# A one-core encoder trunk: how a Strassen FFN transfers its weight sums, and its second column block as a plain product

## The chip, the cores and the metric

The kernel runs on one core of a Trainium2 chip as one launch. The metric is the device time in microseconds (us), the median of three runs.

## The reference

Two requests of 256 tokens each (512 tokens in all, width 1024) go through two layers. A layer is a half-step SwiGLU FFN, a token mixer, and a second half-step FFN; all in float32.

```
def swiglu(x, wg, wu, wd):
    return (jax.nn.silu(x @ wg) * (x @ wu)) @ wd
...
    for l in range(DEPTH):
        x = x + 0.5 * swiglu(rmsnorm(x, ffn1_norm[l]), ffn1_wg[l], ffn1_wu[l], ffn1_wd[l])
        h = rmsnorm(x, mix_norm[l])
        ...
        x = x + merged @ w_out[l]
        x = x + 0.5 * swiglu(rmsnorm(x, ffn2_norm[l]), ffn2_wg[l], ffn2_wu[l], ffn2_wd[l])
```

`wg` and `wu` are 1024 x 2816, `wd` is 2816 x 1024. The four calls of the FFN are named FFN 1 to FFN 4 here, in order of time.

## The kernel before, in words

**Precision.** Each float32 operand is split into a rounded high part and the rest (`split`, lines 218 to 229: ACT copies the high part `wh`, line 226; DVE subtracts it and leaves `wl`, line 228). A product is three matmuls: high x high, high x low, low x high.

**The FFN** (`ffn`, from line 339). The normed input lies transposed in `xT` = (`xth`, `xtl`), 8 slices of 128 channels by 512 tokens. The 22 column tiles of `wg` and `wu` are worked off in pairs, 11 blocks, in three stages (tiles 0 to 7, 8 to 15, 16 to 21); after each stage `rowproj` (lines 295 to 336) multiplies by the matching rows of `wd`. Before, block 0 is a plain product (`proj`, lines 235 to 242: for a 128-column weight tile, 8 slices x 3 matmuls; in block 0 in two halves of 256 tokens). The ten other blocks call `seven` (lines 393 to 443), a Strassen scheme (Winograd form). It takes the weights as a 2 x 2 matrix whose rows are the channel halves and whose columns are gate and up, and the activations as channel halves by token halves. So W11 is the upper half of `wg`, W21 the lower half of `wg`, W22 the lower half of `wu`. It makes seven products of 24 matmuls with 256 columns (`product`, lines 384 to 391), in the order W11, t2, t1, t3, W21, W22, and the second t2; the block ends with vector work for silu and the gate (lines 420 to 443).

**The activation side** (`combos`, lines 355 to 374) is made once in each FFN. Four tiles `q` are filled by a transfer of the high part (SP's queue, line 361) and an accumulating transfer of the low part (POOL's queue, line 362); four subtractions on DVE (line 363) make the sums, and these are split into `C[5]`, `C[6]`, `C[7]`, `C[3]` (lines 370, 371). `C[5]` and the negated `C[4]` are written in place into the second token half of `xT`, so all of `xT` must have been read by then.

**The weight side** in `seven`: the sums t1 and t3 come by transfer. SP loads t1's first addend and W22 into the two halves of a `raw` tile (lines 399, 400), POOL adds the upper half of `wu` onto t1 (line 401); t3 goes as two halves into the tiles P and M, loaded by SP (line 406) and added onto by POOL (line 407). W11 and W21 go in halves into tiles S and R. DVE makes t2 = t1 + W22 (line 416), and adds W21 onto it later (line 431).

**What sets the order.** Every engine and each transfer queue works in the order of its instructions. A scheduler fixes that order when the program is built, from priorities and its own timing. The loads and splits of a block have a priority that puts them up to a block ahead. `raw` has 2 tiles, `wh` and `wl` 4 each, P and M 2 each. A tile is reused when its last reader is done.

Of the kernel before, what the change touches and what calls it, by code (L numbers as in the profile page):

```python
# [13 lines left out]
F32 = mybir.dt.float32  # L14
F32R = mybir.dt.float32r
# [45 lines left out]
def trunk_kernel(tc, I, O, dbg=None, depth=DEPTH, stop=None):  # L61
    nc = tc.nc
    with ExitStack() as st:
# [22 lines left out]
        def uv(shape=(P, 2, TOK), dt=F32):  # L86
            return pv_.tile(list(shape), dt, tag="v", name=nm("v"))
# [4 lines left out]
        def dtmp(tag, shape=(P, H, P)):  # L92
            return pd.tile(list(shape), F32, tag=tag, name=nm(tag))
# [245 lines left out]
        def ffn(wg, wu, wd, xT, after, extra=None, norm=None):  # L339
# [15 lines left out]
            def combos():  # L355
                q = {}
                for g, c in enumerate((g0, g1)):
                    for k, r in enumerate((low, high)):
                        q[g, k] = u((P, 4, 256))
                        with tc.high_priority(offset=100):  # L360
                            nc.sync.dma_start(q[g, k], xh[:, r, c].bitcast(F32))
                            G_.dma_start(q[g, k], xl[:, r, c].bitcast(F32), accum_op=ALU.add)
                sub = lambda o, i, j: V.tensor_tensor(o, i, j, op=ALU.subtract)
                sub(q[1, 1], q[1, 0], q[1, 1])
                sub(q[1, 0], q[1, 0], q[0, 0])
                sub(q[0, 0], q[0, 0], q[1, 1])
                sub(q[0, 1], q[0, 1], q[0, 0])
                for n, f, dst in ((5, q[1, 1], [t[:, low, g1] for t in xT]), (6, q[0, 0], None), (7, q[1, 0], None), (3, q[0, 1], None)):
                    hi, lo = C[n] = dst or [uv((P, 4, 256), F32R) for _ in range(2)]
                    A.copy(hi, f)  # L370
                    V.tensor_tensor(lo, f, hi.bitcast(F32), op=ALU.subtract)  # L371
                C[4] = [t[:, high, g1] for t in xT]
                for t in C[4]:
                    A.activation(t, t.bitcast(F32), AF.Copy, scale=-1.0)
# [9 lines left out]
            def product(ps, w, act, start=True):  # L384
                (wh, wl), (ch, cl) = w, act
                for j in range(2):
                    m, o = slice(j * P, (j + 1) * P), ps[:, j, :]
                    for k in range(4):
                        T.matmul(o, wh[:, k, m], ch[:, k, :], start=start and j + k == 0, stop=False, skip_group_check=True)  # L389
                        T.matmul(o, wh[:, k, m], cl[:, k, :], start=False, stop=False, skip_group_check=True)  # L390
                        T.matmul(o, wl[:, k, m], ch[:, k, :], start=False, stop=k == 3, skip_group_check=True)  # L391

            def seven(f, hh, hl):
                c = slice(f * P, f * P + 256)
                rows = lambda w, k0, n: w[k0 * P:(k0 + n) * P, c].rearrange("(k p) n -> p k n", p=P)
                with tc.high_priority(offset=AHEAD):
                    r = pr.tile([P, 2048], F32, tag="raw", name=nm("raw")).rearrange("p (q k n) -> p q k n", q=2, k=4)
                    w11, w22, t1_ = [dtmp("S", (P, 2, 256)) for _ in range(2)], r[:, 1], r[:, 0]
                    nc.sync.dma_start(t1_, rows(wg, 0, 4))
                    nc.sync.dma_start(w22, rows(wu, 4, 4))  # L400
                    G_.dma_start(t1_, rows(wu, 0, 4), accum_op=ALU.add)
                    for i, t in enumerate(w11):
                        nc.sync.dma_start(t, rows(wg, 2 * i, 2))
                    t3 = [dtmp(n, (P, 2, 256)) for n in "PM"]
                    for i, t in enumerate(t3):
                        nc.sync.dma_start(t, rows(wu, 4 + 2 * i, 2))
                        G_.dma_start(t, rows(wu, 2 * i, 2), accum_op=ALU.add)
                    w21 = [dtmp("R", (P, 2, 256)) for _ in range(2)]
                    for i, t in enumerate(w21):
                        nc.sync.dma_start(t, rows(wg, 4 + 2 * i, 2))  # L410
                sq_ = (P, 2, 256)
                X, E, Z = bank("f", sq_), bank("d", sq_), bank("a", sq_)
                product(X, parts_of(w11), X11)
                with tc.high_priority(offset=AHEAD):
                    t2 = u((P, 4, 256))
                    V.tensor_tensor(t2, t1_, w22, op=ALU.add)
                p1s, G = dtmp("C", sq_), dtmp("E", sq_)
                A.copy(p1s, X)
                product(E, parts_of([t2]), C[6])
                V.tensor_tensor(G, E, p1s, op=ALU.subtract)  # L420
                product(Z, parts_of([t1_]), C[5])
                product(E, parts_of(t3), C[7], False)
                H, y22 = dtmp("B", sq_), tmp(sq_)
                V.tensor_tensor(H, E, p1s, op=ALU.subtract)
                V.tensor_tensor(y22, Z, H, op=ALU.add)
                product(X, parts_of(w21), X12, False)
                s0 = tmp(sq_)
                A.activation(s0, X, AF.Silu)
                with tc.high_priority(offset=AHEAD):
                    for i, t in enumerate(w21):  # L430
                        V.tensor_tensor(t2[:, 2 * i:2 * i + 2, :], t2[:, 2 * i:2 * i + 2, :], t, op=ALU.add)
                product(Z, parts_of([w22]), C[3], False)
                V.tensor_tensor(G, Z, G, op=ALU.add)
                V.tensor_tensor(s0, s0, G, op=ALU.mult)
                product(E, parts_of([t2]), C[4], False)
                y21 = dtmp("B", sq_)
                V.tensor_tensor(y21, p1s, E, op=ALU.subtract)
                A.activation(y21, y21, AF.Silu)
                V.tensor_tensor(y22, y21, y22, op=ALU.mult)
                for v, g in ((s0, g0), (y22, g1)):  # L440
                    hi, lo = hh[-1][:, :, g], hl[-1][:, :, g]
                    A.copy(hi, v)
                    V.tensor_tensor(lo, v, hi.bitcast(F32), op=ALU.subtract)

            for f0, f1 in ((0, 8), (8, 16), (16, 22)):
                hh, hl = [], []
                for f in range(0, f1 - f0, 2):
                    hh.append(u(dt=F32R))
                    hl.append(u(dt=F32R))
                    if f0 + f:  # L450
                        seven(f0 + f, hh, hl)
                        continue
                    bs = [bank_alt() for _ in range(4)]
                    if norm is not None:
                        ws = []
                        norm(0)
                        for i, (b, rv) in enumerate(zip(bs, raw0)):
                            hi = pw.tile([P, 8, P], F32R, tag="whi", name=nm("wh"))
                            lo = pw.tile([P, 8, P], F32R, tag="wlo", name=nm("wl"))
                            if i:  # L460
                                k = (3, 7, 7)[i - 1]
                                A.copy(hi[:, 0, :1], xT[0][:, k, :1])
                                V.tensor_copy(lo[:, 0, :1], xT[1][:, k, :1])
                            ws.append(split(rv, (hi, lo), off=0 if i else AHEAD))
                            proj(b, ws[-1], xT, 0, 256)
                        norm(1, [w[0][:, 0, :1].bitcast(F32) for w in ws])
                        for b, w in zip(bs, ws):
                            proj(b, w, xT, 256, 512)
                    else:
                        gs, us = wcols(wg, 0), wcols(wu, 0)  # L470
                        for g in range(2):
                            for b, w in zip(bs, (gs[0], us[0], gs[1], us[1])):
                                proj(b, w, xT, g * 256, g * 256 + 256)
                    combos()
                    for j in range(2):
                        gate(bs[2 * j], bs[2 * j + 1], f + j, hh, hl)

                if extra is not None and f1 == 22:
                    extra()

                def src(k, hh=hh, hl=hl):
                    return hh[k // 2][:, k % 2, :], hl[k // 2][:, k % 2, :]
                rowproj(src, wd[f0 * P:f1 * P, :], f1 - f0, 0.5, after if f1 == 22 else None, hold=uv)
# [726 lines left out]
```

## Time and profile before

| | |
|---|---|
| median of 3 runs | 2544.05 us (2541.56 to 2551.43) |
| profiled execution, its own time | 2543.35 us |
| span of its profile | 2541.6 us |
| busy PE / DVE / ACT / POOL | 2365.4 / 1501.1 / 1005.3 / 415.4 us |
| mean granted clock of PE | 0.958 |
| moved by DMA | 322.59 MB, mean 127 GB/s |

PE is the matmul engine, DVE, ACT and POOL the vector, scalar and general engines, SP the engine that issues most transfers. In a timeline row the first number is the start in the profile, the second the duration, both us; `[a <-X]` says that the engine had been idle for a us and what ended it. In a row that groups instructions, `x` is the count, then come busy us and the mean ns of one. The granted clock 1.00 is TensorE's level of 2.4 GHz, 0.50 its level of 1.2 GHz. The span leaves some 1.75 us of the execution's own time outside.

### The profile page before, as it was taken

How to read it: one execution, taken by the hardware profiler on the slowest of the kernel's cores; microseconds unless marked ns; L12 is line 12 of the kernel's file. 1: busy time of each engine (PE TensorE's matmuls, PEld its weight loads, DVE VectorE, ACT ScalarE, POOL GpSimd, SP SyncE). 2: the span in 40 equal slices, each digit the busy share in tenths (PEclk: the TensorE clock that was granted, in tenths of full speed). 3: DMA queues.
4: the chain of work that ended last, by engine and by line, in shares of the span. 5: the costliest groups of instructions: out<-in, count | busy, mean ns of one | idle time of the engine just before them, and what ended most of it. 6: DMA issues, size and time to landing. Idle time of an engine off the chain costs nothing.

```text
span 2541.6 us, 37166 instructions
## 1 busy us (share of the span) xinstructions
PE 2365.4 (93%) x14923; PEld 2140.4 (84%) x14923; DVE 1501.1 (59%) x2344; ACT 1005.3 (40%) x1904; POOL 415.4 (16%) x371
## 2 busy tenths in 40 slices
PE   6899999999999979989988989999999999799998
PEld 5889888878899868988878888888888988688897
DVE  4746565577665455565656464655776553656555
ACT  4423344643433343343444242446344333433333
POOL 2011011023341110100020010001343401101000
PEclk8899999999999989999989999999999999899999
DMA  9446435641124465654475545357221246545542
GB/s 252 112 132 155 133 99 184 154 118 57 59 68 142 139 142 143 147 133 118 130 170 130 133 127 139 95 168 181 89 80 51 85 140 159 124 133 133 133 117 75
DMA packets 296605, 322.59 MB, mean 127 GB/s; under 512 B 21869, under 2 KB 261761, under 8 KB 296432
## 3 DMA queue, kind: packets, MB, share of 16 engines
q1 hardware_dynamic: 239648, 251.33, 31.6%
q0 software_dynamic: 56608, 68.68, 15.8%
q8 instruction: 117, 1.92, 0.3%
q14 instruction: 56, 0.46, 0.1%
q10 hardware_dynamic: 176, 0.20, 0.0%
HBM read 292.08 MB, written 11.30 MB: 119 GB/s over the span
## 4 chain that ended last, share of the span: by engine, by line
PE 77%; DVE 9%; DMA 7%; ACT 4%; issue 2%; SPq 1%; POOL 1%; POOLq 0%; DVEq 0%; ACTq 0%
PE ps L389 11%; PE ps L391 11%; PE ps L390 11%; PE ps L298 7%; PE ps L299 7%; PE ps L300 7%; PE ps L241 4%; PE ps L240 4%; PE ps L242 4%; DMA u<-xth 2%; DVE wl L228 2%; ACT wh L226 2%; DMA v<-gcd 1%; PE ps L861 1%; DMA u<-xtl 1%
## 5 line engine op out<-in xcount | busy, mean ns | idle before, releaser
L226 ACT CAST wh<-raw 128x1024 fp32r<-128x1024 f32 x286 | 298.7, 1048 | 472.1 <-PE ps L300 162.5
L228 DVE TENSOR_TENSOR wl<-raw,wh 128x1024 fp32r<-128x1024 f32 x274 | 339.5, 1243 | 229.7 <-ACT wh L226 224.2
L389 PE MATMUL ps<-xth,wh 128*128 128x256 f32 x1280 | 374.3, 293 | 56.2 <-ACT wh L226 21.8
L389 PE MATMUL ps<-v,wh 128*128 128x256 f32 x960 | 295.5, 308 | 84.8 <-ACT wh L226 76.3
L390 PE MATMUL ps<-xtl,wh 128*128 128x256 f32 x1280 | 368.5, 289 | 0.7 <-DVE xtl L371 0.7
L391 PE MATMUL ps<-xth,wl 128*128 128x256 f32 x1280 | 363.7, 287 | 4.7 <-DVE wl L228 4.7
L240 PE MATMUL ps<-xth,wh 128*128 128x512 f32 (+1 forms) x928 | 326.6, 361 | 5.5 <-ACT t L501 2.0
L241 PE MATMUL ps<-xtl,wh 128*128 128x512 f32 (+1 forms) x928 | 329.6, 360 | 1.2 <-DVE xtl L287 1.2
L242 PE MATMUL ps<-xth,wl 128*128 128x512 f32 (+1 forms) x928 | 327.0, 358 | 0.0
L389 PEld LDWEIGHTS ps<-xth,wh 128*128 128x128 f32 x1280 | 252.1, 197 | 65.8 <-ACT wh L226 30.4
L391 PE MATMUL ps<-v,wl 128*128 128x256 f32 x960 | 291.5, 304 | 0.0
L390 PE MATMUL ps<-v,wh 128*128 128x256 f32 x960 | 290.7, 303 | 0.0
L389 PEld LDWEIGHTS ps<-v,wh 128*128 128x128 f32 x960 | 204.4, 213 | 91.8 <-ACT wh L226 82.0
L299 PE MATMUL ps<-wl,u 128*128 128x512 f32 x672 | 261.8, 390 | 0.0
L298 PE MATMUL ps<-wh,u 128*128 128x512 f32 x672 | 261.3, 390 | 0.0
L300 PE MATMUL ps<-wh,u 128*128 128x512 f32 x672 | 260.8, 389 | 0.0
L390 PEld LDWEIGHTS ps<-xtl,wh 128*128 128x128 f32 x1280 | 252.9, 198 | 1.1 <-DVE xtl L371 1.0
L391 PEld LDWEIGHTS ps<-xth,wl 128*128 128x128 f32 x1280 | 248.7, 195 | 5.5 <-DVE wl L228 5.5
L391 PEld LDWEIGHTS ps<-v,wl 128*128 128x128 f32 x960 | 204.5, 213 | 0.2
L390 PEld LDWEIGHTS ps<-v,wh 128*128 128x128 f32 x960 | 204.3, 213 | 0.4
L240 PEld LDWEIGHTS ps<-xth,wh 128*128 128x128 f32 x928 | 175.1, 191 | 31.3 <-ACT t L501 2.4
L241 PEld LDWEIGHTS ps<-xtl,wh 128*128 128x128 f32 x928 | 177.1, 191 | 24.1 <-DVE xtl L287 1.6
(349 smaller groups left out, 4379.0 us busy)
## 6 DMA issues: line engine op xcount, KB each, us to landing
raw<-in_w_in_dram SPq DMA_DIRECT2D x44, 1024.0 KB, 5.1
raw<-in_ffn_wd_dram SPq DMA_DIRECT2D x40, 1024.0 KB, 5.4
raw<-in_ffn_wg_dram SPq DMA_DIRECT2D x40, 512.0 KB, 3.9
raw<-in_ffn_wu_dram SPq DMA_DIRECT2D x40, 512.0 KB, 5.1
raw<-in_ffn_wu_dram POOLq DMA_DIRECT2D x40, 512.0 KB, 6.4
R<-in_ffn_wg_dram SPq DMA_DIRECT2D x80, 256.0 KB, 4.1
S<-in_ffn_wg_dram SPq DMA_DIRECT2D x80, 256.0 KB, 4.5
M<-in_ffn_wu_dram SPq DMA_DIRECT2D x40, 256.0 KB, 2.9
```

What stands on the lines that cost most here:

```text
L226: A.copy(hi, rv)
L228: (G_ if share and turn[0] % 2 else V).tensor_tensor(lo, rv, hi.bitcast(F32), op=ALU.subtract)
L240: T.matmul(o, wh[:, k, m], xh[:, k, c0:c1], start=k == 0, stop=False)
L241: T.matmul(o, wh[:, k, m], xl[:, k, c0:c1], start=False, stop=False)
L242: T.matmul(o, wl[:, k, m], xh[:, k, c0:c1], start=False, stop=k == n - 1)
L298: T.matmul(ps, sh[:, a], wh, start=k == 0, stop=False)
L299: T.matmul(ps, sh[:, a], wl, start=False, stop=False)
L300: T.matmul(ps, sl[:, a], wh, start=False, stop=k == nk - 1)
L389: T.matmul(o, wh[:, k, m], ch[:, k, :], start=start and j + k == 0, stop=False, skip_group_check=True)
L390: T.matmul(o, wh[:, k, m], cl[:, k, :], start=False, stop=False, skip_group_check=True)
L391: T.matmul(o, wl[:, k, m], ch[:, k, :], start=False, stop=k == 3, skip_group_check=True)
L861: T.matmul(pp[:, h, :], lhs[:, h, :], rhs[:, h, :], start=True, stop=True)
```

## The change

It does three things. In `seven`, t3 now has the half of the `raw` tile in which W22 was, with one load and one accumulating transfer; W22 goes in halves into P and M, by plain loads, and the sum t2 is made in two halves. In `ffn`, the second block (tiles 2 and 3) is a plain product over all 512 tokens: four `proj` of 24 matmuls with 512 columns, each pair followed by `gate`; so nine blocks are left for `seven`. And `combos` ends before the in-place writes of `C[5]` and `C[4]`; these stand in a function of their own, which is called after the second block.

```diff
-                for n, f, dst in ((5, q[1, 1], [t[:, low, g1] for t in xT]), (6, q[0, 0], None), (7, q[1, 0], None), (3, q[0, 1], None)):
-                    hi, lo = C[n] = dst or [uv((P, 4, 256), F32R) for _ in range(2)]
+                for n, f in ((6, q[0, 0]), (7, q[1, 0]), (3, q[0, 1])):
+                    hi, lo = C[n] = [uv((P, 4, 256), F32R) for _ in range(2)]
                     A.copy(hi, f)
                     V.tensor_tensor(lo, f, hi.bitcast(F32), op=ALU.subtract)
+                return q[1, 1]
+
+            def in_place(f):
+                hi, lo = C[5] = [t[:, low, g1] for t in xT]
+                A.copy(hi, f)
+                V.tensor_tensor(lo, f, hi.bitcast(F32), op=ALU.subtract)
                 C[4] = [t[:, high, g1] for t in xT]
...
-                    w11, w22, t1_ = [dtmp("S", (P, 2, 256)) for _ in range(2)], r[:, 1], r[:, 0]
+                    w11, w22, t1_ = [dtmp("S", (P, 2, 256)) for _ in range(2)], [dtmp(n, (P, 2, 256)) for n in "PM"], r[:, 0]
+                    t3 = r[:, 1]
                     nc.sync.dma_start(t1_, rows(wg, 0, 4))
-                    nc.sync.dma_start(w22, rows(wu, 4, 4))
-                    G_.dma_start(t1_, rows(wu, 0, 4), accum_op=ALU.add)
+                    nc.sync.dma_start(t3, rows(wu, 4, 4))
+                    for t in (t1_, t3):
+                        G_.dma_start(t, rows(wu, 0, 4), accum_op=ALU.add)
+                    for i, t in enumerate(w22):
+                        nc.sync.dma_start(t, rows(wu, 4 + 2 * i, 2))
                     for i, t in enumerate(w11):
                         nc.sync.dma_start(t, rows(wg, 2 * i, 2))
-                    t3 = [dtmp(n, (P, 2, 256)) for n in "PM"]
-                    for i, t in enumerate(t3):
-                        nc.sync.dma_start(t, rows(wu, 4 + 2 * i, 2))
-                        G_.dma_start(t, rows(wu, 2 * i, 2), accum_op=ALU.add)
...
-                    V.tensor_tensor(t2, t1_, w22, op=ALU.add)
+                    for i, t in enumerate(w22):
+                        V.tensor_tensor(t2[:, 2 * i:2 * i + 2, :], t1_[:, 2 * i:2 * i + 2, :], t, op=ALU.add)
...
-                product(E, parts_of(t3), C[7], False)
+                product(E, parts_of([t3]), C[7], False)
...
-                product(Z, parts_of([w22]), C[3], False)
+                product(Z, parts_of(w22), C[3], False)
...
+                    if f0 + f > 2:
+                        seven(f0 + f, hh, hl)
+                        continue
                     if f0 + f:
-                        seven(f0 + f, hh, hl)
+                        gs, us = wcols(wg, f * P), wcols(wu, f * P)
+                        for j in range(2):
+                            pg, pu_ = bank_alt(), bank_alt()
+                            proj(pg, gs[j], xT)
+                            proj(pu_, us[j], xT)
+                            gate(pg, pu_, f + j, hh, hl)
+                        in_place(d5)
                         continue
...
-                    combos()
+                    d5 = combos()
```

The scheduler orders the changed program anew. Three places of that order:

DVE at the start of FFN 2, before: the rows around the first subtraction (`L363`), which waits for the transfers into the tiles `q` (named `u` in the rows).

```order
L343 TENSOR_TENSOR t1208_8125<-t1208_8125,ps1185_7878 128x512
L346 TENSOR_TENSOR u1183_7876<-t1208_8125,u1182_7875 128x512
L416 TENSOR_TENSOR u1224_8188<-raw1212_8137 128x1024
L363 TENSOR_TENSOR u1201_8102<-u1200_8099,u1201_8102 128x1024
L228 TENSOR_TENSOR wl1228_8194<-u1224_8188,wh1227_8193 128x1024
L343 TENSOR_TENSOR t1209_8130<-t1209_8130,ps1187_7880 128x512
L363 TENSOR_TENSOR u1200_8099<-u1200_8099,u1198_8093 128x1024
L228 TENSOR_TENSOR wl1230_8223<-raw1212_8137,wh1229_8222 128x1024
```

The same place of the changed program:

```order
L228 TENSOR_TENSOR wl1199_8019<-raw1197_8016,wh1198_8018 128x1024
L363 TENSOR_TENSOR u1186_7985<-u1185_7982,u1186_7985 128x1024
L343 TENSOR_TENSOR t1193_8004<-t1193_8004,ps1170_7761 128x512
L228 TENSOR_TENSOR wl1201_8023<-raw1197_8016,wh1200_8022 128x1024
L363 TENSOR_TENSOR u1185_7982<-u1185_7982,u1183_7976 128x1024
L346 TENSOR_TENSOR u1168_7759<-t1193_8004,u1167_7758 128x512
L228 TENSOR_TENSOR wl1204_8029<-raw1202_8026,wh1203_8028 128x1024
L363 TENSOR_TENSOR u1183_7976<-u1183_7976,u1186_7985 128x1024
```

`raw1197` and `raw1202` hold the second block's columns of `wg` and `wu`. Only the first of its four weight tiles is split ahead of the waiting subtraction; the tile that the second `proj` reads (`wl1204`) stands five rows behind it. FFN 4 has the same order.

DVE at the start of FFN 3, in the changed program:

```order
L228 TENSOR_TENSOR wl1660_11466<-raw1658_11463,wh1659_11465 128x1024
L343 TENSOR_TENSOR t1654_11451<-t1654_11451,ps1631_11208 128x512
L228 TENSOR_TENSOR wl1662_11470<-raw1658_11463,wh1661_11469 128x1024
L346 TENSOR_TENSOR u1629_11206<-t1654_11451,u1628_11205 128x512
L363 TENSOR_TENSOR u1647_11432<-u1646_11429,u1647_11432 128x1024
L228 TENSOR_TENSOR wl1665_11476<-raw1663_11473,wh1664_11475 128x1024
L363 TENSOR_TENSOR u1646_11429<-u1646_11429,u1644_11423 128x1024
```

Here two tiles are split ahead of the subtraction, and the one for the second `proj` (`wl1665`) stands right behind it. In FFN 1 three of the four stand ahead, and the fourth is the next row.

POOL's queue at the start of FFN 2, before:

```order
L362 DMA u1198_8093<-xtl1155_7716 128x4x256
L362 DMA u1199_8096<-xtl1155_7716 128x4x256
L247 TENSOR_TENSOR nr1175_7833<-nst1174_7831,mhalf_114 128x1
L407 DMA P1215_8145<-in_ffn2_wu_dram 128x2x256
L407 DMA P1248_8394<-in_ffn2_wu_dram 128x2x256
L401 DMA raw1245_8386<-in_ffn2_wu_dram 128x4x256
L362 DMA u1200_8099<-xtl1155_7716 128x4x256
L362 DMA u1201_8102<-xtl1155_7716 128x4x256
```

In the changed program the last two transfers into the tiles `q` are followed, not preceded, by the accumulations of weights:

```order
L362 DMA u1185_7982<-xtl1140_7599 128x4x256
L362 DMA u1186_7985<-xtl1140_7599 128x4x256
L409 DMA raw1215_8152<-in_ffn2_wu_dram 128x4x256 x2
L409 DMA raw1248_8401<-in_ffn2_wu_dram 128x4x256 x2
```

Three transfers (256, 256 and 512 KB) have left their place ahead. The mixer of layer 0 is also ordered anew: among its 490 instructions on DVE, 204 stood otherwise than in layer 1 before; now the two layers' mixers have one order, which is that of layer 1 before but for 6 rows.

## Rows read from the trace of the kernel before

**Rows 1.** The page's chain that ended last: share of the span by engine, then by line.

```profile
PE 77%; DVE 9%; DMA 7%; ACT 4%; issue 2%; SPq 1%; POOL 1%; POOLq 0%; DVEq 0%; ACTq 0%
PE ps L389 11%; PE ps L391 11%; PE ps L390 11%; PE ps L298 7%; PE ps L299 7%; PE ps L300 7%; PE ps L241 4%; PE ps L240 4%; PE ps L242 4%; DMA u<-xth 2%; DVE wl L228 2%; ACT wh L226 2%; DMA v<-gcd 1%; PE ps L861 1%; DMA u<-xtl 1%
```

**Rows 2.** The same chain in order of time (start us, us, what), at the starts of FFN 1, 2, 3 and 4: the transfers into the tiles `q`.

```profile
37.79 17.74 DMA u<-xth
56.12 7.25 DMA u<-xtl
...
889.45 14.72 DMA u<-xth
...
906.25 7.17 DMA u<-xtl
...
1309.06 7.19 DMA u<-xtl
...
2142.81 14.71 DMA u<-xth
...
2159.40 7.35 DMA u<-xtl
```

**Rows 3.** Busy time in stretches: the stretch, its length, PE, PE's weight loads, DVE, ACT, POOL (each busy us and count), granted clock, DMA share, GB/s. In this order: 40 us of the down projection (512 columns); the second and the third stage's Strassen blocks of FFN 1 (four and three); the first stage's three Strassen blocks of FFN 1, 2, 3 and 4, from the end of the plain block to the end of the last; the mixers of layers 0 and 1.

```profile
140.00:180.00 40.00, 40.00 (x178) 33.10 (x178) 18.46 (x23) 9.70 (x12) 2.56 (x2) 1.00 0.46 121
182.90:277.40 94.50, 86.07 (x674) 84.74 (x673) 59.92 (x79) 38.59 (x56) 12.22 (x10) 0.95 0.58 146
320.90:392.40 71.50, 65.68 (x508) 64.75 (x506) 46.75 (x65) 33.78 (x48) 8.48 (x12) 0.93 0.39 104
...
40.00:139.40 99.40, 71.81 (x506) 69.30 (x506) 59.53 (x74) 38.13 (x52) 12.27 (x10) 0.81 0.64 151
904.20:997.80 93.60, 72.58 (x524) 69.98 (x523) 59.66 (x75) 38.62 (x53) 11.12 (x9) 0.85 0.53 129
1309.00:1395.40 86.40, 68.81 (x506) 66.92 (x505) 57.02 (x70) 35.99 (x50) 9.84 (x8) 0.88 0.55 130
2157.00:2247.10 90.10, 67.96 (x506) 66.17 (x506) 59.01 (x73) 38.23 (x52) 11.12 (x9) 0.85 0.55 129
426.90:832.90 406.00, 396.20 (x2376) 345.28 (x2376) 257.31 (x507) 181.82 (x471) 115.13 (x95) 0.99 0.35 104
1683.00:2085.80 402.80, 395.28 (x2377) 345.50 (x2376) 254.87 (x506) 182.87 (x471) 110.52 (x95) 0.99 0.36 105
```

**Rows 4.** The timeline of PE: the longest wait at the starts of FFN 1, 2, 3 and 4.

```profile
51.60 0.58 PE L389 MATMUL ps<-xth,wh 128*128 128x256 f32 x1 [11.60 <-ACT wh L226]
...
915.87 0.58 PE L389 MATMUL ps<-xth,wh 128*128 128x256 f32 x1 [8.74 <-ACT xth L370]
...
1319.40 0.58 PE L389 MATMUL ps<-xth,wh 128*128 128x256 f32 x1 [7.48 <-ACT C L418]
...
2169.20 0.58 PE L389 MATMUL ps<-xth,wh 128*128 128x256 f32 x1 [9.21 <-ACT xth L370]
```

**Rows 5.** The timeline of PE at the seam of two Strassen blocks of FFN 1: two rows 49 matmuls apart, then the wait, and behind it two rows 24 matmuls apart, the second the first at the old pace.

```profile
110.02 0.28 PE L391 MATMUL ps<-xth,wl 128*128 128x256 f32 x1
...
115.90 0.28 PE L391 MATMUL ps<-xth,wl 128*128 128x256 f32 x1
118.82 0.58 PE L389 MATMUL ps<-v,wh 128*128 128x256 f32 x1 [2.64 <-ACT wh L226]
...
120.15 0.41 PE L390 MATMUL ps<-xtl,wh 128*128 128x256 f32 x1
...
125.27 0.31 PE L389 MATMUL ps<-xth,wh 128*128 128x256 f32 x1
```

**Rows 6.** Groups of instructions by line over the whole span: the split's subtraction, its copy, the sum t2, and the subtractions of `combos`; then from DVE's timeline one row of the gate's product.

```profile
L228 DVE TENSOR_TENSOR wl<-raw,wh 128x1024 fp32r<-128x1024 f32 x274 | 339.5, 1243 | 229.7 <-ACT wh L226 224.2 <-PE ps L517 4.8
...
L226 ACT CAST wh<-raw 128x1024 fp32r<-128x1024 f32 x286 | 298.7, 1048 | 472.1 <-PE ps L300 162.5 <-PE ps L390 145.3 <-PE ps L241 99.4
...
L416 DVE TENSOR_TENSOR u<-raw 128x1024 f32<-128x1024 f32 x40 | 48.8, 1219 | 29.3 <-DMA raw<-in_ffn_wu_dram 29.3
...
L363 DVE TENSOR_TENSOR u<-u,u 128x1024 f32<-128x1024 f32 x16 | 19.5, 1219 | 23.5 <-DMA u<-xtl 23.4
...
915.79 0.68 DVE L343 TENSOR_TENSOR t<-t,ps 128x512 f32<-128x512 f32 x1
```

**Rows 7.** Busy time in stretches, as rows 3: the transfers while those into the tiles `q` are under way, in FFN 2 and in FFN 1.

```profile
880.00:905.00 25.00, 24.58 (x203) 24.13 (x203) 7.12 (x15) 6.92 (x16) 7.12 (x7) 1.00 1.10 253
40.00:50.00 10.00, 0.00 (x1) 0.00 (x0) 1.83 (x3) 0.00 (x0) 1.93 (x2) 0.67 1.18 238
```

**Rows 8.** Transfers by line over the whole span: queue, count, KB each, median us from issue to landing; then from POOL's timeline the accumulations at the start of FFN 2.

```profile
raw<-in_ffn_wg_dram SPq DMA_DIRECT2D x40, 512.0 KB, 3.9
raw<-in_ffn_wu_dram SPq DMA_DIRECT2D x40, 512.0 KB, 5.1
raw<-in_ffn_wu_dram POOLq DMA_DIRECT2D x40, 512.0 KB, 6.4
...
u<-xtl POOLq DMA_DIRECT2D x16, 512.0 KB, 9.0
...
883.24 3.01 POOL L407 DMA_DIRECT2D P<-in_ffn_wu_dram x2
888.67 1.29 POOL L401 DMA_DIRECT2D raw<-in_ffn_wu_dram x1 [2.42 <-issue]
```

## The prediction

> **What bounds the kernel now.** I read the chain that ended last first [rows 1]: 77% of it is matmuls, and of the rest the transfers into the tiles `q` are the one entry that a single place explains. The same chain in order of time shows that place [rows 2]: at the start of each FFN, PE has finished the plain first block and waits until the activation sums are made. PE's timeline has the longest of these waits [rows 4]: 11.60, 8.74, 7.48 and 9.21 us, each ended by a split behind the sums. Smaller waits follow, and after a wait TensorE runs at its lower level for a while. In the seam of two blocks [rows 5] 49 matmuls took 5.88 us before the wait, 0.120 us each (2.4 GHz), and 24 took 5.12 us behind it, 0.213 us each (1.2 GHz); the old pace is back 6.45 us after the start, so such a wait costs some 6.45 x 0.44 = 2.8 us on top of itself. Last I read the stretches [rows 3]: the first stage's three Strassen blocks take 99.4, 93.6, 86.4 and 90.1 us, while three of the third stage take 71.5. The stretch of FFN 2 has 18 matmuls of the down projection in it (524 against 506), 18 x 0.227 = 4.1 us, so it counts 89.5. The four sum to **365.4 us**.
>
> **The part that is taken out and put in.** Of each first stage, three Strassen blocks become a plain block and two Strassen blocks.
>
> The plain block is 96 matmuls with 512 columns. The down projection has 178 rows in 40.00 us, two of them cut by the edges [rows 3]: 0.227 us each, so 21.8 us if PE never waits. A Strassen block is 168 x 0.120 = 20.2 us of matmuls [rows 5], so the plain one costs PE 1.6 us more; what it avoids is waiting.
>
> Two Strassen blocks: four in a row take 94.5 us, 13.7 over their matmuls (80.8), for three seams; three take 71.5, 10.9 over 60.6, for two seams [rows 3]. A seam so costs 4.6 to 5.5 us; I take 5.0. Two blocks with one seam are 40.4 + 5.0 = 45.4 us; the upper bound is two thirds of 71.5, 47.7.
>
> Without waits, the stretch is 21.8 + 45.4 = 67.2 us, four times 268.8, which is **96.6 us less** than now.
>
> **What is late next.** DVE works in order, and the changed order puts splits of the second block's weights behind the first subtraction of `combos`, which waits for the last transfer into the tiles `q`. So I need when that lands, counted from the end of the first block. Now [rows 2, 3]: FFN 1 at 63.4, 23.4 us after its 40.0; FFN 2 at 913.4, 9.2 after; FFN 3 at 1316.25, 7.2 after; FFN 4 at 2166.75, 9.7 after.
>
> In the change the accumulations of weights that stood ahead on POOL follow later. In FFN 2 they are three [rows 8], 1.05 MB. All transfers were saturated there, 238 to 253 GB/s [rows 7], so without them the rest is through 4.4 us earlier by bytes. In FFN 1 six such accumulations, 2.1 MB, no longer stand ahead of the last transfer or among it, which is 8.8 us; the next block's loads (1.05 MB) may come beside it and take back up to 4.4. The least is no gain at all, as if the loads alone set the time. I take the bytes: landings 4.8 (FFN 2), 2.8 (FFN 3), 5.3 (FFN 4), and for FFN 1 the middle, 16.8.
>
> FFN 2 and 4: behind the landing stand two subtractions of 1.22, one gate product of 0.68, one 512-wide split of the gate at the same length, and two splits of 1.24 before the second `proj` has its weights' low part [rows 6], about 6.0 us when packed: at 10.8 and 11.3. PE needs it at the third matmul of that `proj`, 26 x 0.227 = 5.9. So PE waits 4.9 and 5.4 us, plus 2.8 for the clock: 7.7 and 8.2. FFN 3: one subtraction and one split, 2.4 us, so at 5.2, before 5.9: no wait. FFN 1: the fourth weight tile, needed after 74 matmuls at 16.8, is there at 16.8 + 2.4 = 19.2; 2.4 us, and I count 3 for a partial fall of the clock. Sum of the waits **18.9 us**; bounds are 0 and, with today's landings, 11.8 + 12.1 + 6.5 + 12.8 = 43.2.
>
> The sums themselves stay hidden. In FFN 2, four subtractions and three splits of `combos` are done some 12 us behind the landing, at 17; `C[6]` is needed after the plain block and one product, at 24 us or later. The in-place part needs the plain block's end: a copy of 1.05 and a split of 1.24 [rows 6], 2.3 us, while PE has two products of 24 matmuls (5.8 us) that do not read it. Without that cover it would cost 2.3 in each FFN.
>
> **The transfers of weights.** The bytes of a Strassen block stay the same; three accumulations become two, off the path (POOL is busy 415 us). t2 in two halves costs about 0.07 us more than one of 1.22 [rows 6]; it stands in the seam of each of 36 blocks: 2 us. The splits of t3 and W22 change places, halves against whole, and even out. W11's loads are now queued on SP behind W22's halves; the halves' tiles come free in the block two before, so a block of time (over 20 us) covers a transfer of 4 to 5 us. If that cover were gone, PE would wait at each block's start.
>
> **The mixer.** Layer 0's mixer takes the order of layer 1's. They take 406.0 and 402.8 us now [rows 3]; I count 3 us less, between none and 6.
>
> **Sum.** 96.6 - 18.9 - 2 + 3 = 78.7 us less. The profiled execution took 2543.35 us by its own time (1.75 more than its span), 0.7 under the median of the three runs. That makes **2464.7**; I say 2465.
>
> **Rivals.**
> *All hidden* (0.22): the transfers land 5 us earlier than I take them, and no split is late: 2543.35 - 96.6 + 2 - 3 = 2446. For it: the two last accumulations are then alone, and they carry 1.05 MB in about 7.2 us [rows 2], 146 GB/s, far under the 238 of the crowded stretch. Against it: they were nearly alone before too. The Trainium skill's page "DMA: Bandwidth & Descriptors", section "Anatomy of one DMA — SWDGE (gpsimd) path", has a fit of 2.0 us plus bytes over 436 GB/s; for 512 KB that is an estimate of 3.2 us where the row has 7.2, and by it the splits would be almost in time, which is this rival. The median of these transfers here is 9.0 us and of the weights' 6.4 [rows 8], so the traces speak for the longer time.
>
> *No earlier landing* (0.17): the loads ahead of the sums, not the accumulations, set the landing. Waits of 43.2 and pairs of 47.7 (9 us more): 2543.35 - 96.6 + 43.2 + 9 + 2 - 3 = 2498.
>
> *A new wait in every block* (0.05, slower): both sums now share one `raw` tile, and t2 needs two more loads. Should t2 come to wait for its accumulation in each block, as it did 8 times for 29.3 us [rows 6], 3.7 each, then 36 blocks pay 133 us, plus the clock: 2465 + 133 = 2598 at least. It decides from 2.2 us a block on (78.7 / 36). Against it: a `raw` tile comes free a block and a half, some 35 us, before t2 needs it again, and load and accumulation take 5.1 + 6.4 us [rows 8]; t3 is split earlier in the block than W22 was, so the tile comes free earlier too.
>
> *The second block does not hide the sums* (0.04, same): the scheduler leaves the waiting subtraction ahead of the splits in all four FFNs and the landing comes as late as in FFN 1: four waits of some 22 us, net within 12 us of now. The order shows it otherwise for FFN 1 and 3.
>
> **How the numbers follow.** The forecast has 0.48. Between it and its neighbours lies the remaining 0.04. The range 2443 to 2498 takes in the first two rivals and the forecast with its bounds. A change of under 0.5% (12.7 us) can hardly be told from none here. Faster by more: 0.22 + 0.48 + 0.17 + 0.04 = 0.91; same 0.04; slower 0.05.
>
> **What would show it.** After: the last transfer into the tiles `q` lands about 4.8, 2.8 and 5.3 us after the first block in FFN 2, 3 and 4. In FFN 2 and 4, PE has one wait of about 5 us at the second `proj` of the plain block, ended by a split; in FFN 3 none. The first stage takes 70 us in FFN 1, 75 in FFN 2 and 4, 67 in FFN 3. The seams of the other blocks keep waits of 1.6 to 3.6 us. Wrong if PE waits for the sums behind the plain block, if the seams grow, or if t2 waits for a transfer in most blocks.

## The result, and the profile after

The changed kernel takes **2460.72 us** (median of 3 runs, 2460.06 to 2461.69) against 2544.05: a ratio of **0.9667**, 95% interval 0.9635 to 0.9698. Forecast were 2465 us and faster with 0.91. The profiled execution went from a span of 2541.6 to 2458.9 us, 82.7 less.

The stretches that answer to [rows 3], from the profile after (columns as there). In this order: the first stage of FFN 1 from the end of the plain first block to the first matmul of the down projection; the second and third stage of FFN 1; the mixer with what lies around it, layer 0; the first stages of FFN 2 and 3; the same mixer stretch of layer 1; the first stage of FFN 4.

```profile
39.77:112.48 72.71, 67.08 (x433) 62.40 (x432) 49.78 (x62) 33.91 (x47) 6.41 (x5) 0.93 0.65 160
156.02:249.44 93.42, 85.27 (x674) 83.92 (x673) 60.36 (x82) 39.09 (x56) 5.18 (x4) 0.96 0.52 138
292.83:364.66 71.83, 65.61 (x508) 64.69 (x507) 46.80 (x67) 33.74 (x48) 7.39 (x11) 0.93 0.38 105
396.33:802.36 406.03, 397.90 (x2396) 348.04 (x2393) 256.94 (x511) 185.43 (x476) 106.81 (x93) 0.99 0.35 105
873.80:945.70 71.90, 65.66 (x434) 59.92 (x432) 49.23 (x61) 33.29 (x46) 5.18 (x4) 0.95 0.61 150
1261.31:1333.74 72.43, 65.62 (x434) 60.74 (x432) 46.85 (x59) 30.25 (x42) 5.17 (x4) 0.95 0.60 150
1618.26:2025.79 407.53, 398.56 (x2395) 348.32 (x2393) 258.32 (x511) 185.41 (x476) 106.92 (x93) 0.99 0.36 105
2097.14:2165.98 68.84, 64.60 (x433) 59.68 (x433) 49.19 (x62) 32.28 (x45) 5.17 (x4) 0.98 0.60 152
```

The four first stages sum to 72.71 + 71.90 + 72.43 + 68.84 = 285.9 us, where they were 365.4: **79.5 of the 82.7 us are there**. The second and third stage of FFN 1 stand within 1.1 us of [rows 3].

In PE's timeline the long waits of [rows 4] are gone. The waits of over 0.5 us inside the plain blocks, and in FFN 1 inside the first Strassen block, are now these:

```profile
66.25 0.40 PE L395 MATMUL ps<-v,wh 128*128 128x256 f32 x1 [1.83 <-ACT wh L226]
67.51 0.58 PE L397 MATMUL ps<-v,wl 128*128 128x256 f32 x1 [0.64 <-DVE wl L228]
...
882.25 0.80 PE L240 MATMUL ps<-xth,wh 128*128 128x512 f32 x1 [2.98 <-ACT wh L226]
884.66 0.80 PE L242 MATMUL ps<-xth,wl 128*128 128x512 f32 x1 [1.19 <-DVE wl L228]
...
1271.98 0.80 PE L242 MATMUL ps<-xth,wl 128*128 128x512 f32 x1 [4.75 <-DVE wl L228]
...
2105.52 0.50 PE L242 MATMUL ps<-xth,wl 128*128 128x512 f32 x1 [1.67 <-DVE wl L228]
```

DVE's timeline at the start of FFN 2 shows why (bracket: how long DVE stood idle before the row, and for what); behind it the first subtraction of FFN 1, 3 and 4:

```profile
866.64 1.23 DVE L228 TENSOR_TENSOR wl<-raw,wh 128x1024 fp32r<-128x1024 f32 x1 [8.36 <-ACT wh L226]
878.78 1.23 DVE L363 TENSOR_TENSOR u<-u,u 128x1024 f32<-128x1024 f32 x1 [10.91 <-DMA u<-xtl]
879.92 0.68 DVE L343 TENSOR_TENSOR t<-t,ps 128x512 f32<-128x512 f32 x1
880.52 1.22 DVE L228 TENSOR_TENSOR wl<-raw,wh 128x1024 fp32r<-128x1024 f32 x1
881.65 1.22 DVE L363 TENSOR_TENSOR u<-u,u 128x1024 f32<-128x1024 f32 x1
882.79 0.69 DVE L346 TENSOR_TENSOR u<-t,u 128x512 fp32r<-128x512 f32 x1
883.39 1.22 DVE L228 TENSOR_TENSOR wl<-raw,wh 128x1024 fp32r<-128x1024 f32 x1
...
50.96 1.23 DVE L363 TENSOR_TENSOR u<-u,u 128x1024 f32<-128x1024 f32 x1 [7.02 <-DMA u<-xtl]
...
1269.57 1.23 DVE L363 TENSOR_TENSOR u<-u,u 128x1024 f32<-128x1024 f32 x1 [10.71 <-DMA u<-xtl]
...
2099.63 1.23 DVE L363 TENSOR_TENSOR u<-u,u 128x1024 f32<-128x1024 f32 x1 [8.43 <-DMA u<-xtl]
```

The subtraction stands on DVE for 10.91 us until its transfer has landed, and the split that ends at 884.6 is the one that PE waits for at 884.66. The wait of 2.98 us ahead of it has the same cause by way of ACT: there the copy of the gate waits for DVE's row at 879.92, and the copy of the weights that PE needs stands behind it.

```profile
880.63 0.62 ACT L345 CAST u<-t 128x512 fp32r<-128x512 f32 x1 [11.15 <-DVE t L343]
881.16 1.04 ACT L226 CAST wh<-raw 128x1024 fp32r<-128x1024 f32 x1
```

The last landings are 11.2, 5.0, 8.3 and 2.5 us behind the first block (which ends at 39.77, 873.80, 1261.31 and 2097.14). POOL's timeline shows that the accumulations start earlier: in FFN 2 the last two are issued 3.8 us before the end of the first block, where they were 0.5 and 2.0 behind it (first the row of the profile after, then the two of the profile before).

```profile
870.00 2.63 POOL L362 DMA_DIRECT2D u<-xtl  x2 [16.61 <-issue]
...
904.76 1.27 POOL L362 DMA_DIRECT2D u<-xtl  x1 [14.80 <-DVE t L343]
906.25 1.28 POOL L362 DMA_DIRECT2D u<-xtl  x1 [0.22 <-issue]
```

The accumulations of xtl themselves are no faster: their median is 10.1 us here and 8.7 in a second profile of this kernel, against 9.0 in [rows 8]. What has become faster are the loads of xth, on whose landing POOL issues them: 8.2 us instead of 12.8 (three rows of the profile after, then the load's of the profile before).

```profile
raw<-in_ffn_wu_dram POOLq DMA_DIRECT2D x72, 512.0 KB, 7.5
...
u<-xth SPq DMA_DIRECT2D x16, 512.0 KB, 8.2
u<-xtl POOLq DMA_DIRECT2D x16, 512.0 KB, 10.1
...
u<-xth SPq DMA_DIRECT2D x16, 512.0 KB, 12.8
```

### The profile page after: what moved, and what is told of

It reads as the page before. It is cut to its first block, busy times and chain, and to the rows that moved or that the text cites. A ratio compares the mean times of both kernels' runs of the same rounds, so it can differ in the third digit from the quotient of the medians.

```text
span 2458.9 us, 36338 instructions
## 1 busy us (share of the span) xinstructions
PE 2350.2 (96%) x14635; PEld 2114.2 (86%) x14635; DVE 1460.9 (59%) x2324; ACT 989.9 (40%) x1876; POOL 353.2 (14%) x323
## 2 busy tenths in 40 slices
DMA packets 289306, 316.24 MB, mean 129 GB/s; under 512 B 20718, under 2 KB 254466, under 8 KB 289137
## 5 line engine op out<-in xcount | busy, mean ns | idle before, releaser
L240 PE MATMUL ps<-xth,wh 128*128 128x512 f32 (+1 forms) x1056 | 377.9, 365 | 8.7 <-ACT wh L226 3.5
L242 PE MATMUL ps<-xth,wl 128*128 128x512 f32 (+1 forms) x1056 | 378.6, 363 | 7.6 <-DVE wl L228 7.6
L241 PE MATMUL ps<-xtl,wh 128*128 128x512 f32 (+1 forms) x1056 | 381.5, 365 | 1.2 <-DVE xtl L287 1.2
L395 PE MATMUL ps<-xth,wh 128*128 128x256 f32 x1152 | 330.6, 288 | 8.3 <-ACT wh L226 7.9
L396 PE MATMUL ps<-xtl,wh 128*128 128x256 f32 x1152 | 326.9, 285 | 0.0
L397 PE MATMUL ps<-xth,wl 128*128 128x256 f32 x1152 | 322.1, 283 | 0.0
L395 PE MATMUL ps<-v,wh 128*128 128x256 f32 x864 | 263.0, 304 | 60.3 <-ACT wh L226 60.3
L396 PE MATMUL ps<-v,wh 128*128 128x256 f32 x864 | 260.2, 301 | 0.0
L395 PEld LDWEIGHTS ps<-v,wh 128*128 128x128 f32 x864 | 182.0, 211 | 65.7 <-ACT wh L226 65.4
L242 PEld LDWEIGHTS ps<-xth,wl 128*128 128x128 f32 x1056 | 201.6, 191 | 37.8 <-DVE wl L228 9.2
L409 POOL DMA_DIRECT2D raw<-in_ffn_wu_dram x72 | 93.2, 1342 | 957.9 <-DMA raw<-in_ffn_wg_dram 752.2
L397 PEld LDWEIGHTS ps<-xth,wl 128*128 128x128 f32 x1152 | 219.9, 192 | 0.0
```

The lines of the kernel that those rows point to most:

```text
L240: T.matmul(o, wh[:, k, m], xh[:, k, c0:c1], start=k == 0, stop=False)
L241: T.matmul(o, wh[:, k, m], xl[:, k, c0:c1], start=False, stop=False)
L242: T.matmul(o, wl[:, k, m], xh[:, k, c0:c1], start=False, stop=k == n - 1)
L409: G_.dma_start(t, rows(wu, 0, 4), accum_op=ALU.add)
```

## Experiments

Theory: the plain block covers the sums, and what is left of the waits are splits that stand on DVE behind the waiting subtraction. Rivals: the gain comes from the new transfers; the sums are merely late elsewhere; and, for the price of the plain block itself, that it pays only as a cover. The first four kernels share one set of runs of the kernel before (2546.27 us), the next four another (2548.09), the last two a third (2545.43).

**The change once more.**

> The changed kernel once more, as the yardstick for the other three: 2461 us, 0.967 of the time before, first stages of 73, 72, 73 and 69 us.

2454.72 us, 0.9636 (0.9616 to 0.9657); first stages 73.14, 72.24, 66.08 and 69.03. FFN 3 has **no wait** in its plain block in this execution: its last transfer landed 2.9 us behind the first block instead of 8.3. The same kernel took 2460.06 to 2461.69 us in one set of runs and 2453.91 to 2455.16 in the other. In the profiles, FFN 3's first stage is 6.35 us shorter in the second, but its first block ended 3.0 later; another 3.0 lie in layer 1's mixer. What is known of FFN 3 is below; why the sets differ stays open.

**The plain block alone.** Against the change, `seven` has its old transfers:

```diff
-                    t3 = r[:, 1]
-                    nc.sync.dma_start(t3, rows(wu, 4, 4))
-                    for t in (t1_, t3):
-                        G_.dma_start(t, rows(wu, 0, 4), accum_op=ALU.add)
+                    nc.sync.dma_start(w22, rows(wu, 4, 4))
+                    G_.dma_start(t1_, rows(wu, 0, 4), accum_op=ALU.add)
...
+                    for i, t in enumerate(t3):
+                        nc.sync.dma_start(t, rows(wu, 4 + 2 * i, 2))
+                        G_.dma_start(t, rows(wu, 2 * i, 2), accum_op=ALU.add)
```

> The second block is a plain product, and the transfers of the Strassen blocks are those of the kernel before. Theory (the plain block that covers the sums is the whole gain; the new transfers are worth nothing by themselves): 2455 to 2470 us, the first stages 67 to 76 us each, the seams as before. Rival (sharing the raw tile is what lets the last transfer into the tiles q land earlier): the landings stay at 23, 9, 7 and 10 us behind the first block, PE waits in the plain block of all four FFNs for some 43 us in sum, and it takes about 2490 us.

2468.68 us, 0.9689 (0.9663 to 0.9714): most of the gain is the plain block's, yet it is 14 us slower than the change, so the first theory holds only in the main. The landings are near the rival's 23, 9, 7 and 10 (19.1, 8.3, 7.7 and 8.5 us behind the first block), but PE's waits come to 20.8 us, and in FFN 1 not in the plain block, where it had 43 (with the clock's part) in all four plain blocks:

```profile
70.11 0.58 PE L395 MATMUL ps<-v,wh 128*128 128x256 f32 x1 [5.66 <-ACT wh L226]
...
890.35 0.80 PE L242 MATMUL ps<-xth,wl 128*128 128x512 f32 x1 [5.34 <-DVE wl L228]
...
1280.59 0.80 PE L242 MATMUL ps<-xth,wl 128*128 128x512 f32 x1 [4.23 <-DVE wl L228]
...
2118.98 0.80 PE L242 MATMUL ps<-xth,wl 128*128 128x512 f32 x1 [5.61 <-DVE wl L228]
```

**The transfers alone.** The kernel before, with the change's `seven` and no plain second block.

> The transfers of the change, and the second block stays a Strassen block as before. Theory (the transfers are worth nothing by themselves: the same bytes, t2 in two halves costs 0.07 us more in 40 blocks): 2540 to 2550 us, PE waits of 7 to 12 us stay behind the first block of each FFN. Rival (the shared raw tile brings the sums' transfers forward): the waits behind the first block shrink by 4 us or more each, 2515 to 2530 us.

2552.84 us, 1.0021 (1.0006 to 1.0035): some 5 us slower, where 3 were expected (40 x 0.07), and 3 us above the expected range. PE still waits behind the first block:

```profile
50.99 0.58 PE L389 MATMUL ps<-xth,wh 128*128 128x256 f32 x1 [10.22 <-ACT wh L226]
...
922.83 0.58 PE L389 MATMUL ps<-xth,wh 128*128 128x256 f32 x1 [8.39 <-ACT xth L370]
...
1329.42 0.58 PE L389 MATMUL ps<-xth,wh 128*128 128x256 f32 x1 [9.54 <-ACT C L419]
...
2180.24 0.58 PE L389 MATMUL ps<-xth,wh 128*128 128x256 f32 x1 [9.19 <-ACT xth L370]
```

So the rival of shorter waits is wrong: the transfers cost a little by themselves and gain 14 us only together with the plain block. The loads of xth go the same way: a median of 13.8 us here and 9.9 with the plain block alone, against 12.8 before and 8.2 with both.

**The splits first.** The four weight tiles of the second block are asked for ahead of the sums, and the first subtraction is made to depend on the last of their splits.

```diff
-                        gs, us = wcols(wg, f * P), wcols(wu, f * P)
...
-                    d5 = combos()
+                    gs, us = wcols(wg, 2 * P), wcols(wu, 2 * P)
+                    one = small("one", (1,))
+                    with tc.high_priority(offset=AHEAD):
+                        V.tensor_scalar(one, us[1][1][:, 0, :1].bitcast(F32), 0.0, 1.0, op0=ALU.mult, op1=ALU.add)
+                    d5 = combos(one)
...
-                sub(q[1, 1], q[1, 0], q[1, 1])
+                V.scalar_tensor_tensor(q[1, 1], q[1, 0], one, q[1, 1], op0=ALU.mult, op1=ALU.subtract)
```

> The change, with the four splits of the second block's weights put ahead of the first subtraction of the sums on DVE (a number that the subtraction needs is made from the last split's result). Theory (what is left of the waits are those splits, standing behind a subtraction that waits for its transfer): the waits of 2.98 and 1.19 (FFN 2), 4.75 (FFN 3) and 1.67 us (FFN 4) inside the plain block go, and with them 3.1, 1.6 and 1.1 us at the lower clock, 16 us in all: 2445 us, plain blocks of 22.0 us in all four FFNs. Rival (the cover then ends too early): the raw tiles come free earlier, the third block's loads and accumulations run beside the last transfer of the sums and hold it up (landing 8 us or more behind the first block in FFN 2 and 4 too, where the change has 5.0 and 2.5), and PE waits at the first Strassen block instead, as in FFN 1 (2.5 us and some 3 us of clock): 2455 to 2465 us.

2445.76 us, 0.9600 (0.9576 to 0.9624): 9 us less than the change on the same chip. Expected were 16, reckoned from the first profile, whose FFN 3 still had 6 us to lose. The plain blocks of FFN 1 to 4, and the two Strassen blocks of FFN 2:

```profile
39.79:61.74 21.95, 21.95 (x100) 18.19 (x99) 12.85 (x16) 8.46 (x13) 6.42 (x5) 1.00 1.15 251
873.64:895.59 21.95, 21.95 (x100) 18.19 (x99) 14.55 (x17) 8.03 (x11) 5.17 (x4) 1.00 1.18 245
1257.73:1279.68 21.95, 21.95 (x100) 18.18 (x99) 18.20 (x22) 10.68 (x14) 5.20 (x4) 1.00 1.13 235
2084.44:2106.39 21.95, 21.95 (x100) 18.19 (x99) 15.31 (x18) 9.23 (x12) 5.14 (x4) 1.00 1.17 241
895.59:938.99 43.40, 40.99 (x336) 40.37 (x336) 33.64 (x44) 23.64 (x33) 0.00 (x0) 1.00 0.40 123
```

PE is busy for the whole of each plain block. The rival's mechanism is there too, and harmless: DVE goes on from the transfer only 15.5, 8.3, 4.2 and 7.1 us behind the first blocks, where the change's first profile has 11.2, 5.0, 8.3 and 2.5, and at the first Strassen block PE waits as in the change's second profile (2.25 and 0.76 us in FFN 1 against 2.23 and 0.70, elsewhere none over 0.5).

**Once more, as yardstick.**

> The change with the second block's splits ahead of the first subtraction, once more as the yardstick for the others: 0.960 of the time before, 2445 us.

2444.58 us, 0.9593 (0.9573 to 0.9613).

**The sums of the high parts alone.** In `combos`:

```diff
-                            G_.dma_start(q[g, k], xl[:, r, c].bitcast(F32), accum_op=ALU.add)
```

> The change, with the sums made of the high parts alone: the four accumulating transfers of xtl into the tiles q are left out in each FFN, so the sums lack the low parts. Theory (a split is late only because the subtraction ahead of it waits for that transfer): the sums are there before the first block ends in FFN 2 to 4, no wait inside the plain block, 22.0 us each, in FFN 1 none at the first Strassen block either; 2440 to 2446 us, like the version with the splits first. Rival (the splits are late by the loads of their weights or by the order on ACT): waits of 3 to 6 us stay in the plain blocks of FFN 2 to 4, 2455 us or more.

2440.40 us, 0.9579 (0.9560 to 0.9599). The plain blocks of FFN 2 to 4 take 21.8 us, busy throughout; FFN 1 has one wait of 0.90 there and none at the first Strassen block. Without the late transfer the splits of FFN 2 to 4 are in time, although all four stand behind the first subtraction on DVE: both, the wait and what stands behind it, are needed for the loss.

**Old transfers, plain block, splits first.** The two edits above together.

> The transfers of the kernel before, the plain second block, and its splits ahead of the first subtraction. Theory (when the last transfer lands matters only through the splits that stand behind the subtraction on DVE): landings at 8 us and more behind the first block as without the new transfers, but plain blocks of 22.0 us in all four FFNs; 2446 to 2453 us, some 20 us less than the plain block with the old transfers alone (2469); FFN 1 keeps its wait of 5 to 6 us at the first Strassen block. Rival (the old accumulations on POOL hold up the sums so far that PE waits for them behind the plain block): waits of 5 us or more at the first Strassen block in every FFN, 2462 to 2470 us.

2448.29 us, 0.9618 (0.9594 to 0.9642), by the ratios of both 18 us less than the plain block alone ((0.9689 - 0.9618) x 2547), though the transfers let DVE go on as late as 18.1, 9.3, 9.6 and 9.0 us behind the first block. Plain blocks of FFN 2 to 4:

```profile
877.02:898.81 21.79, 21.79 (x98) 18.03 (x98) 14.36 (x16) 7.36 (x10) 2.59 (x3) 1.00 0.97 196
1257.67:1279.47 21.80, 21.80 (x99) 18.04 (x98) 14.02 (x16) 7.38 (x10) 2.58 (x2) 1.00 0.97 195
2085.99:2107.78 21.79, 21.79 (x99) 18.03 (x98) 14.49 (x16) 7.39 (x11) 3.51 (x3) 1.00 0.96 196
```

Its interval overlaps that of the new transfers with the same order, so a difference between the two sets of transfers is then no longer resolved. **In the plain blocks an earlier landing is worth something only where splits stand behind the subtraction.** In FFN 1 it counts in one more place: there t2 stands on DVE behind the sums, and PE waits for its split at the first Strassen block 4.79 us here, 2.25 with the new transfers and not at all with the high parts alone.

**Every block plain.**

```diff
-                    if f0 + f > 2:
-                        seven(f0 + f, hh, hl)
-                        continue
...
-                        gs, us = wcols(wg, f * P), wcols(wu, f * P)
+                        gs, us = wcols(wg, (f0 + f) * P), wcols(wu, (f0 + f) * P)
...
-                        in_place(d5)
...
-                    d5 = combos()
```

> Every block of every FFN a plain product; no sums, no Strassen block. Theory (the prices of the forecast: a plain block is 96 x 0.229 = 21.95 us, a Strassen block with its seam 23.6, since four took 93.4 to 96.3 us and three about 71.3): second stages 87.8 instead of 95.2, third stages 65.9 instead of 71.3, first stages 65.9 instead of 71.6 us behind the first block; 18.5 us less in each FFN than in the change, 74 in all, 2385 us. Rival (a plain block hides its own weights only while Strassen blocks stand behind it: four splits a block, each waiting for a tile of the block before, leave a wait of 2 to 3 us a block, as the seams have now): 40 x 2.5 = 100 us back, 2470 to 2490 us.

**2376.21 us, 0.9327 (0.9309 to 0.9345)**, which beats both kernels: 3.2% under the change (0.9327 / 0.9636), and 9 us under the expected 2385. The three stages of FFN 1 and the first of FFN 2, and the page's first row:

```profile
39.85:105.03 65.18, 65.18 (x288) 53.84 (x288) 26.09 (x29) 22.81 (x31) 0.00 (x0) 1.00 0.35 113
148.72:235.59 86.87, 86.87 (x384) 71.93 (x384) 29.34 (x31) 24.60 (x31) 0.00 (x0) 1.00 0.31 97
279.28:344.54 65.26, 65.26 (x291) 54.00 (x290) 24.21 (x25) 20.33 (x25) 0.00 (x0) 1.00 0.32 99
852.46:917.61 65.15, 65.15 (x290) 53.92 (x289) 22.45 (x24) 18.75 (x24) 0.00 (x0) 1.00 0.33 107
...
PE 2347.7 (99%) x12043; PEld 1991.9 (84%) x12043; DVE 1099.5 (46%) x1752; ACT 823.5 (35%) x1598; POOL 239.1 (10%) x235
```

In these stretches PE never waits and the granted clock is 1.00. Against the change each stage is shorter: 86.9 against 93.4, 65.3 against 71.8. The rival, that a plain block can't have its weights ready for the next, is wrong: DVE needs 29.3 us of the 86.9. By these stretches a plain block is 1.6 to 2.2 us cheaper than a Strassen block with its seam (6.55 / 4 and 6.57 / 3). So an estimate is that 7 to 9 of the 79.5 us that the change saves in four first stages are the plain block's own price; the rest is the waiting that it covers.

**Every block plain, in halves of 256 columns.**

```diff
-                            proj(pg, gs[j], xT)
-                            proj(pu_, us[j], xT)
+                            for g in range(2):
+                                proj(pg, gs[j], xT, g * 256, g * 256 + 256)
+                                proj(pu_, us[j], xT, g * 256, g * 256 + 256)
```

> Every block a plain product as before, but each in two halves of 256 columns (192 matmuls a block instead of 96). Theory (what a Strassen block saves in products it pays back in narrower matmuls and seams: 0.120 us for 256 columns against 0.227 for 512): 192 x 0.120 = 23.0 us a block against 21.8, 40 blocks, 48 us more than with 512 columns, 2424 us; the Strassen block's 168 x 0.120 = 20.2 saves its eighth only against these 23.0. Rival (the width costs nothing; the 13 ns above 0.107 are the seams' lower clock): within 10 us of the version with 512 columns, 2376 to 2386 us.

2425.68 us, 0.9530 (0.9504 to 0.9556), 48 us over the version with 512 columns on the same chip. The second stage of FFN 1, with 768 matmuls where that has 384:

```profile
153.24:245.23 91.99, 91.99 (x769) 91.99 (x769) 29.32 (x31) 24.40 (x31) 0.00 (x0) 1.00 0.29 92
```

91.99 / 768 = 0.120 us for 256 columns, 86.87 / 384 = 0.226 for 512, both at 2.4 GHz and without a wait: 256 columns cost 53% of 512. The Trainium skill's page "TensorE: Matmul & The Clock Gate", section "Wait — 56ns, not 53.3ns?", gives N / 2.4 GHz + 2.5 ns between starts of back-to-back matmuls. An estimate from that, for 96 more matmuls, is 0.24 us a block or 10 us for 40 blocks, the rival's bound. The rows here, where each matmul has a weight load of its own, show some 13 ns instead of 2.5, and the runs 48 us; the measurement decides.

**That yardstick.**

> Every block a plain product with 512 columns, once more as the yardstick: 0.933 of the time before, 2376 us.

2377.44 us, 0.9340 (0.9315 to 0.9365).

## Why the prediction was right, step by step

**What bounds the kernel.** Right. 79.5 of 82.7 us come from the four first stages, 77.7 were forecast there (96.6 - 18.9).

**The two prices.** The plain block without waits was put at 21.8 us; with the splits first it takes 21.79 from its first matmul to the next block's (the stretches of 21.95 above reach 0.16 us into it). The pair of Strassen blocks was put at 45.4 in all four; from start to start FFN 2 to 4 have 43.0, 44.5 and 44.5. In FFN 1 it took 51.1: PE waits 1.83 and 0.64 us for the split of t2 (rows at 66.25 and 67.51), 1.1 us longer than the others in the seam, and the clock takes its part. t2's two halves stand on DVE behind the sums, which the forecast had down as hidden. The 268.8 without waits came out within 1 us, but by luck: with the splits first the stages take 72.3 (without 18 matmuls of the down projection), 65.2, 66.1 and 66.1 us, 269.7, where each was put at 67.2; FFN 1 is 5 too long, still with its waits for t2, and the others are 1 to 2 too short.

**What is late next.** The mechanism, splits behind the waiting subtraction, is shown by the order (splits first) and by the transfer (high parts alone); each takes the waits away. The sizes, stage by stage: forecast 70, 75, 67 and 75, measured 72.7, 71.9, 72.4 and 68.8, in sum 287.7 and 285.9. The sum was right partly because single errors cancelled:

- FFN 1: the landing came at 11.2 instead of 16.8, so the wait of 3 in the plain block did not come; the 51.1 of the pair stands in its place.
- FFN 2: landing 5.0 against 4.8. The gain by bytes (4.4 us) was right in size: the accumulations are issued 4.3 us earlier with respect to the first block's end. With the old transfers, where two accumulations of weights still stand ahead of them on POOL, the landing is 8.3. The one wait of 4.9 for a split is two, 2.98 for a copy on ACT and 1.19 for the split.
- FFN 3: 8.3 against 2.8, hence a wait of 4.75 where none was forecast. In the second profile of the same kernel it landed at 2.9, without a wait, as forecast. In both, POOL issues the last accumulations when the loads of xth have landed, at 1257.50 and 1257.23; but the first block ended 3.0 us sooner in the first (1261.31 against 1264.31). In the second PE waits 2.10 us in that block for rows normed by a factor that POOL makes (`nr`, line 247); it stands on POOL behind an accumulation that waits for its xth until 1241.37, in the first only until 1239.01. And a split done on DVE before the wait gives a `raw` tile free, so the third block's loads start beside the accumulations, at 1258.29 in the first profile and at 1261.29 in the second; the last accumulation took 10.8 us from its issue in the first and 8.7 in the second. The rows of the first profile, SP's queue and POOL's:

```profile
1257.50 2.62 POOL L362 DMA_DIRECT2D u<-xtl  x2 [13.16 <-DMA u<-xth]
...
1258.29 0.37 SPq L406 DMA_DIRECT2D raw<-in_ffn_wg_dram  x1
1258.71 0.50 SPq L407 DMA_DIRECT2D raw<-in_ffn_wu_dram  x1
```

How the 2.1 us are shared between the loads and chance stays open; no run takes those loads alone away.

- FFN 4: landing 2.5 against 5.3, wait 1.67 against 5.4.

**The clock.** Forecast 2.8 us on top of each wait. FFN 2's plain block took 29.26 us, 3.1 more than 21.95 and its two waits of 4.17; after 4.75 in FFN 3 it was 1.6, after 1.67 in FFN 4 1.1, of which 0.5 is a further wait, for ACT. Right in FFN 2 alone: the term was too large for single waits.

**t2 and the transfers.** Forecast 2 us more. The transfers alone show 5, interval 1.5 to 9, which takes it in. The group that answers to t2 in [rows 6] now has 33.7 us of waiting for a transfer, in 9 of 36 blocks, instead of 29.3 in 8, so the rival of a new wait in every block is wrong:

```profile
L423 DVE TENSOR_TENSOR u<-raw,P 128x512 f32<-128x512 f32 x36 | 24.7, 687 | 33.7 <-DMA raw<-in_ffn_wu_dram 33.7
```

**The mixer.** 3 us less in layer 0: 408.7 to 406.0 in the stretch above, as forecast. Layer 1's went from 405.5 to 407.5, which was not, so the two give 0.7 in all. In the second profile of the changed kernel the same stretches take 405.3 and 404.6: it differs from itself by 3 us in layer 1, so a term of 3 us is not shown by one profile of each.

**The rivals.** *All hidden* (2446) is what the splits-first version measures (2445.8): its price was right, and one order on DVE away, though its landings did not come and the 5 us too many of FFN 1 are in it. *No earlier landing* (2498) had its landings come true with the old transfers (8 to 9 us in FFN 2 to 4), but that took 2469: its 43.2 us of waits were too dear (12.6 in it, not 12.8, would be FFN 4's by its own terms; and there FFN 2 to 4 split two tiles ahead of the subtraction, and FFN 1 waits only at the first Strassen block). *The second block does not hide the sums*: the four waits of some 22 us are nowhere.

**What it overlooked.** Its own numbers, 21.8 for a plain block and 94.5 / 4 = 23.6 for a Strassen block with its seam, say that the plain one is cheaper everywhere. It wrote that what a plain block avoids is waiting for the sums, and did not ask of the other 36. The runs do: 2376 us.

## What to carry to other kernels

Price a scheme that saves products by its stretches, seams included, against the plain product in its widest form: here an eighth fewer columns came to 20.2 against 21.8 us of matmuls, since they were half as wide, and the seam of 5 us ate that three times over. Work that waits for a transfer should stand on an in-order engine behind what the bound engine needs next; then it matters less when the transfer lands (in FFN 2 to 4 here hardly at all).

## What the runs showed of the hardware that was not expected

With no seams, the granted clock over the whole span was 0.997; with 36 Strassen blocks it was 0.974, and 0.93 to 0.98 in the stages whose waits were 1.6 to 4.8 us. The accumulating transfers of 512 KB into the tiles `q` took a median of 10.1 and 8.7 us in two profiles of the change, with other transfers under way. The Trainium skill's page "DMA: Bandwidth & Descriptors", section "Anatomy of one DMA — SWDGE (gpsimd) path", whose fit gives 3.2 us as an estimate, does not hold for them. With every block plain the kernel moves 242.36 MB instead of the change's 316.24.
